# The scores of an indexer tile computed one tile ahead of its search, the first tile's in another buffer

## The chip, the cores and the metric

The kernel runs on one core of a Trainium2 chip. The metric is device time in microseconds (us), the median of the runs. One further execution was profiled, and all rows below are from it.

## The reference, cut to what matters

One step of a two-layer encoder over 592 tokens: 16 meta tokens and 512 prompt tokens (group i), and 64 sample tokens with a cache of 256 keys (group ii). Each layer has three branches. The change touches branch A alone, sparse attention behind an indexer:

```python
s_idx = relu(einsum('bthd,bsd->bths', qib, ki))       # 4 indexer heads of 64
score = einsum('bth,bths->bts', wib, s_idx)
score = where(k_chunk[None, :] <= qcb[:, None], score, -inf)
top_val, top_idx = lax.top_k(score, topk)             # 128 of the prompt's keys, 80 of the sample's
# softmax attention of 8 heads over the chosen keys alone
```

Branch B is a width-4 convolution and a gated linear recurrence (RG-LRU), branch C multi-scale pooling. Every projection is split into a high and a low part and takes three matmuls a step.

## The kernel before

**The main stream.** A layer projects chunk after chunk (`c_project`, 24 accumulating matmuls for each of two pieces of 296 or 288 columns, all on line 255, tile `acc`, three PSUM buffers). The order in the stretch that matters: two indexer query groups QI, four recurrence groups XB, four key groups K, four query groups Q, then the gates GB of branch B. A weight chunk is split by ACT (`wh`, L191) and DVE (`wl`, L192) three chunks ahead of its use. The result of a K or Q group is copied to SBUF by ACT and then gets its rotary part in `rope`: DVE shuffles (L354), POOL multiplies twice (L355 and L356), DVE adds (L357, into `QK`).

**Work at the side.** Generators in the list `side` (indexer and attention) and in `side_lru` (the recurrence of one group, L639 to L675: convolution into `lxc`, two gate matmuls `pg` on L653, ACT functions, two scans L671 and L672) are stepped a little after each piece of a projection. A scheduler then orders the instructions of each engine; every engine works through its own list in that order.

**The indexer.** `index(j)` handles one tile of 128 queries, j = 0 to 3, or the 64 sample queries, j = 4. For each of four heads a matmul (L432, L433 or L435, into `pq`, two PSUM buffers) is followed by a weighted ReLU that adds into the tile `sc` (L438, L442 on DVE, with ACT's ReLU into the tile `rel` between). Then the search repeats two DVE instructions, 16 times (10 for the sample): MAX finds the eight largest of a row, MATCH_REPLACE takes them out. In the profile a MATCH_REPLACE is two rows, MATCH_VALUE_LOAD and MATCH_REPLACE8. Tile 4 is 320 wide, tile 0 is 144 wide and 64 partitions high (partitions 64 to 127), tile 1 is 272 wide. The result is the tile `bias`, which attention adds to its logits. `sc` has one buffer, so the first score row of a tile (L438) waits for the last reader of `sc` of the tile before (L455).

**Who waits for DVE.** `attend_meta` (L596, layer 0 alone) and `attend(4)` (L500) read the `QK` that the L357 adds complete; `attend(4)` reads it through two copies on POOL (L474, into `VI`). A gate's piece leaves PSUM by L695 on DVE (tile `e`), and TensorE reuses that `acc` buffer three pieces later. Under TensorE's in-order list a matmul that waits holds all the matmuls behind it.

In row names PE is TensorE's matmul, DVE VectorE, ACT ScalarE, POOL GpSimd.

Of the kernel before, what the change touches and what calls it, by code (L numbers as in the profile page):

```python
# [9 lines left out]
F32 = mybir.dt.float32  # L10
# [7 lines left out]
NM = 16  # L18
# [49 lines left out]
def build(ctx, tc, ap):  # L68
# [9 lines left out]
    tmp = pool("tmp", 1)  # L78
# [48 lines left out]
    side = Side(RATE_ATT)  # L127
# [169 lines left out]
    def layer(l, xn, x_src, last):  # L297
# [61 lines left out]
        def rotated(ch, dst, pieces):  # L359
            def ev(i, c0, n, p):  # L360
                nc.scalar.activation(dst[:, c0:c0 + n], p, AF.Copy)
            c_project(ch, 8, xn, pieces, ev)
            rope(dst, pieces[0][0])
# [44 lines left out]
        def kspan(j):  # L408

            w = NM + 128 * (j + 1)  # L410
            if w <= 512:
                return [(0, w)]
            return [(0, w // 2), (w // 2, w // 2)]

        def index(j):
            sample = j == 4
            rows = 128
            q0 = NP if sample else NM + 128 * j
            w = 320 if sample else NM + 128 * (j + 1)
            sc = tmp.tile([128, 528], F32, name="sc", tag="sc")  # L420
            spans = [(0, 320)] if sample else kspan(j)
            nq = 64 if sample else 128
            for par in range(2):
                o = 64 * par
                for z in range(0, 128, nq):
                    nc.gpsimd.tensor_copy(qiz[o:o + 64, par::2, z:z + nq], QI[o:o + 64, 0:2, q0:q0 + nq])
            for h in range(4):
                q = qiz[:, h]
                for a, n in spans:
                    p = psq.tile([128, 512], F32, name="pq", tag="qk")  # L430
                    if sample:
                        nc.tensor.matmul(p[:, 0:256], lhsT=q, rhs=kx, start=True, stop=True)  # L432
                        nc.tensor.matmul(p[:, 256:320], lhsT=q, rhs=QI[:, 2, NP:NT], start=True, stop=True)  # L433
                    else:
                        nc.tensor.matmul(p[:, :n], lhsT=q, rhs=QI[:, 2, a:a + n], start=True, stop=True)  # L435
                    wh = wq[:rows, j, h:h + 1]
                    if h == 0:
                        nc.vector.tensor_scalar(sc[:rows, a:a + n], p[:rows, :n], 0.0, wh, op0=ALU.max, op1=ALU.mult)  # L438
                    else:
                        r = tmp.tile([128, 400], F32, name="rel", tag="rel")  # L440
                        nc.scalar.activation(r[:rows, :n], p[:rows, :n], AF.Relu)
                        nc.vector.scalar_tensor_tensor(sc[:rows, a:a + n], r[:rows, :n], wh, sc[:rows, a:a + n],  # L442
                                                       op0=ALU.mult, op1=ALU.add)
                yield w * 1.1
            if not sample:
                nc.gpsimd.memset(sc[0:64, w - 64:w], MASKED)  # L446
            r0 = 64 if j == 0 else 0
            rr = slice(r0, rows)
            m8 = sm.tile([128, 8], F32, name="m8", bufs=2)
            for _ in range(10 if sample else 16):  # L450
                nc.vector.max(m8[rr], sc[rr, :w])  # L451
                nc.vector.match_replace(sc[rr, :w], m8[rr], sc[rr, :w], TAKEN)  # L452
                yield w * 2.1 + 140
            b = lp.tile([128, 528], BF16, name="bias", tag="bias")
            nc.vector.tensor_scalar(b[rr, :w], sc[rr, :w], TAKEN, -1.0e30, op0=ALU.not_equal, op1=ALU.mult)  # L455
            if j == 0:
                nc.vector.memset(b[0:64, 0:w - 64], 0.0)
                nc.vector.memset(b[0:64, w - 64:w], -1.0e30)
            bias[j] = b
            yield w  # L460
# [311 lines left out]
        last_values()  # L772
        for i in range(2):
            rotated(s["c"][C_QI + i], QI[:, i], FULL)
        side.add(index(4))
        side.add(index(0))
        side.add(index(1))
        for g in range(4):
            c_project(s["c"][C_XB + g], 8, xn, FULL, ev_pad(XB[:, g], 3))
            side_lru.add(lru(g))  # L780
# [7 lines left out]
            side.add(attend_meta())  # L788
        side.add(attend(4))
        side.add(attend(0))  # L790
        side.add(index(2))
        side.add(attend(1))
        side.add(index(3))
        side.add(attend(2))
        side.add(attend(3))
        y = new_y()
# [92 lines left out]
    for t, (c0, rows) in enumerate(TILES):  # L889
# [9 lines left out]
        else:  # L899
            norm_T(x[t], rows, c0, r, (g0[:, 0:512], g0[:, 512:1024]), *xn)  # L900
    xn = layer(0, xn, ap["xin"], False)
    layer(1, xn, x1, True)


# [73 lines left out]
```

## Time and profile before

| | |
|---|---|
| median of 3 runs | 1241.58 us (1241.14 to 1242.72) |
| profiled execution, its own time | 1241.46 us |
| its span, first to last instruction | 1239.6 us |
| busy: PE, DVE, ACT, POOL | 1217.6, 731.9, 466.7, 321.4 us |
| mean granted TensorE clock | 0.997 of full speed |

The span plus 1.9 us is the execution's own time. A busy share of an engine is an average over the whole span; in a stretch it can be quite different.

### The profile page before, as it was taken

What the parts mean: (1) busy time and instruction counts of PE and PEld (TensorE: products, weight loads), DVE (VectorE), ACT (ScalarE), POOL (GpSimd) and SP (SyncE); (2) the same over time, 40 slices, a digit from 0 to 9 for tenths busy, and PEclk for the clock granted to TensorE, in tenths of its full rate; (3) what the DMA queues carried; (4) which work ended last, traced back from release to release, by engine and by line L of the source; (5) the groups of instructions that cost most, each with busy time, mean ns of one, the idle gap of its engine ahead of it and who ended that gap; (6) DMA issues with size and microseconds to landing.
All of it is one profiled execution on the core that took longest, in us unless ns stands there. A gap on an engine that the chain in (4) does not pass through costs nothing.

```text
span 1239.6 us, 20846 instructions
## 1 busy us (share of the span) xinstructions
PE 1217.6 (98%) x8314; PEld 1158.5 (93%) x8314; DVE 731.9 (59%) x1502; ACT 466.7 (38%) x913; POOL 321.4 (26%) x428
## 2 busy tenths in 40 slices
PE   9999899999999999999999998899999999999997
PEld 7999889999999999998799998899999999999975
DVE  6268995856954435343453789959497543344332
ACT  6345455333233323332343446443423432233322
POOL 2133454131144400011012334441221442101121
PEclk9999999999999999999999999999999999999999
DMA  8322231221222132222353222222122212222212
GB/s 284 121 74 69 91 108 55 69 69 60 91 76 68 57 93 82 85 74 81 114 160 117 69 68 97 89 69 69 52 94 77 79 52 91 76 81 86 86 35 77
DMA packets 39155, 106.79 MB, mean 86 GB/s; under 512 B 8177, under 2 KB 11313, under 8 KB 38802
## 3 DMA queue, kind: packets, MB, share of 16 engines
q1 hardware_dynamic: 38912, 105.40, 26.4%
q8 instruction: 65, 1.06, 0.3%
q14 instruction: 32, 0.26, 0.1%
q10 hardware_dynamic: 146, 0.07, 0.0%
HBM read 94.83 MB, written 10.09 MB: 85 GB/s over the span
## 4 chain that ended last, share of the span: by engine, by line
PE 87%; DVE 8%; issue 1%; DMA 1%; POOL 1%; ACT 1%; SPq 0%; POOLq 0%; DVEq 0%; ACTq 0%
PE acc L255 75%; PE pq L504 3%; PE pv L547 3%; PE pT L532 2%; DVE wl L192 1%; PE pq L435 1%; DVE sc L452 1%; DVE m L451 1%; DVE lxc L643 1%; DVE rt L354 1%; DVE QK L357 1%; PE pg L761 1%; DMA xi<-xin 1%; PE pT L564 1%; DVE CH L671 1%
## 5 line engine op out<-in xcount | busy, mean ns | idle before, releaser
L255 PE MATMUL acc<-xh,wh 128*128 128x296 f32 (+1 forms) x1728 | 528.5, 306 | 2.8 <-DVE e L695 2.8
L255 PE MATMUL acc<-xh,wl 128*128 128x296 f32 (+1 forms) x1728 | 523.3, 303 | 0.0
L255 PE MATMUL acc<-xl,wh 128*128 128x296 f32 (+1 forms) x1728 | 519.0, 300 | 0.0
L255 PEld LDWEIGHTS acc<-xh,wh 128*128 128x128 f32 x1728 | 326.7, 189 | 6.8 <-DVE e L695 3.0
L255 PEld LDWEIGHTS acc<-xl,wh 128*128 128x128 f32 x1728 | 326.8, 189 | 3.3
L255 PEld LDWEIGHTS acc<-xh,wl 128*128 128x128 f32 x1728 | 325.5, 188 | 2.0
L192 DVE TENSOR_TENSOR wl<-wr,wh 128x1024 fp32r<-128x1024 f32 (+1 forms) x158 | 208.9, 1327 | 200.5 <-ACT wh L191 194.0
L191 ACT ACTIVATE wh<-wr 128x1024 fp32r<-128x1024 f32 (+1 forms) x158 | 166.0, 1053 | 233.8 <-PE acc L255 189.3
L255 PE MATMUL acc<-yh,wh 128*128 128x296 f32 (+1 forms) x384 | 116.9, 304 | 0.0
L255 PE MATMUL acc<-yl,wh 128*128 128x296 f32 (+1 forms) x384 | 115.6, 301 | 0.0
L255 PE MATMUL acc<-yh,wl 128*128 128x296 f32 (+1 forms) x384 | 115.6, 301 | 0.0
L517 POOL TENSOR_SCALAR lpa<-lpa,mn 128x128 f32<-128x128 f32 (+4 forms) x72 | 81.8, 1136 | 109.4 <-DVE mn L516 100.6
L451 DVE MAX8 m<-sc 64x8 f32<-64x144 f32 (+4 forms) x148 | 74.7, 505 | 3.6 <-POOL sc L446 0.7
L255 PEld LDWEIGHTS acc<-yl,wh 128*128 128x128 f32 x384 | 72.2, 188 | 1.3 <-issue 0.2
L255 PEld LDWEIGHTS acc<-yh,wl 128*128 128x128 f32 x384 | 72.2, 188 | 1.2 <-issue 0.4
L255 PEld LDWEIGHTS acc<-yh,wh 128*128 128x128 f32 x384 | 72.3, 188 | 1.0
L452 DVE MATCH_REPLACE8 sc<-m,sc 64x144 f32<-64x144 f32 (+4 forms) x148 | 72.6, 490 | 0.2
L734 POOL TENSOR_TENSOR e<-m,e 128x592 f32<-128x592 f32 (+1 forms) x16 | 23.2, 1450 | 184.4 <-DVE e L728 184.4
L514 ACT ACTIVATE lpa<-lpa,mn 128x144 f32<-128x144 f32 (+4 forms) x72 | 41.2, 572 | 75.0 <-DVE mn L508 74.9
L719 ACT ACTIVATE e<-acc 128x296 f32<-128x296 f32 (+1 forms) x96 | 38.9, 405 | 65.0 <-PE acc L255 64.8
L255 PE MATMUL acc<-wh,ml 128*128 128x512 f32 (+2 forms) x160 | 63.2, 395 | 0.0
L255 PE MATMUL acc<-wh,mh 128*128 128x512 f32 (+2 forms) x160 | 62.8, 394 | 0.0
(209 smaller groups left out, 1639.9 us busy)
## 6 DMA issues: line engine op xcount, KB each, us to landing
wr<-wc SPq DMA_DIRECT2D x108, 512.0 KB, 3.5
wr<-wb SPq DMA_DIRECT2D x24, 512.0 KB, 3.5
wr<-wo SPq DMA_DIRECT2D x16, 512.0 KB, 3.8
kT<-QK SPq DMA_DIRECT2D x2, 1184.0 KB, 4.3
xi<-xin SPq DMA_DIRECT2D x8, 256.0 KB, 7.0
wr<-wv SPq DMA_DIRECT2D x4, 512.0 KB, 6.1
v_p<-VI SPq DMA_DIRECT2D x16, 128.0 KB, 2.1
xo<-xin SPq DMA_DIRECT2D x8, 256.0 KB, 3.1
```

The source lines that it names most:

```text
L191: nc.scalar.activation(h[:, :size], r[:, :size], AF.Copy)
L192: nc.vector.tensor_sub(lo[:, :size], r[:, :size], h[:, :size].bitcast(F32))
L255: nc.tensor.matmul(out, lhsT=a, rhs=b, start=(i == 0), stop=(i == n - 1))
L451: nc.vector.max(m8[rr], sc[rr, :w])
L452: nc.vector.match_replace(sc[rr, :w], m8[rr], sc[rr, :w], TAKEN)
L504: nc.tensor.matmul(p[:, :n], lhsT=qz[u // 2 % 2][:, u % 2], rhs=QK[:, 4 + u // 2, a:a + n], start=True, stop=True)
L514: nc.scalar.activation(t[:, :w], t[:, :w], AF.Exp, bias=mn[:, i:i + 1], scale=-1.0, accum_out=mn[:, 2:3])
L517: nc.gpsimd.tensor_scalar(t[:, :wm], t[:, :wm], mn[:, 3:4], None, op0=ALU.mult)
L532: nc.tensor.transpose(ps[:, k], t[:, 128 * k:128 * k + 128], ident)
L547: nc.tensor.matmul(pvs[i // 2][:, i % 2], lhsT=val(k, i), rhs=pt[:, k], start=(k == 0 and i % 2 == 0), stop=(k == nb - 1), skip_group_chec ...
L719: nc.scalar.activation(e[:, c0:c0 + nn], p, AF.Tanh, scale=0.5)
L734: nc.gpsimd.tensor_tensor(e[:, C0:], m[:, j, C0:], e[:, C0:], op=ALU.add)
```

## The change

`index(j)` is cut in two generators. `scores(j)` computes the scores, `search(j)` searches them. In the list the scores of tile 0 now stand ahead of the search of tile 4, and the scores of tile 1 ahead of the search of tile 0. The scores of tile 0 go into the buffer of the tag `pt`, which attention uses later, all others into `sc` as before. No instruction is added or removed; the lines of the profile move by 3 (L438 becomes L441, L442 L445), by 9 from the search on (L357 keeps its number, L451 becomes L460, L452 L461, L643 L652, L695 L704), and by 14 behind the list.

```diff
--- before.py
+++ after.py
@@ -412,12 +412,15 @@
                 return [(0, w)]
             return [(0, w // 2), (w // 2, w // 2)]
 
-        def index(j):
+        score = {}
+
+        def scores(j):
             sample = j == 4
             rows = 128
             q0 = NP if sample else NM + 128 * j
             w = 320 if sample else NM + 128 * (j + 1)
-            sc = tmp.tile([128, 528], F32, name="sc", tag="sc")
+
+            sc = score[j] = tmp.tile([128, 528 if j else 1024], F32, name="sc", tag="sc" if j else "pt")
             spans = [(0, 320)] if sample else kspan(j)
             nq = 64 if sample else 128
             for par in range(2):
@@ -444,6 +447,12 @@
                 yield w * 1.1
             if not sample:
                 nc.gpsimd.memset(sc[0:64, w - 64:w], MASKED)
+
+        def search(j):
+            sample = j == 4
+            rows = 128
+            w = 320 if sample else NM + 128 * (j + 1)
+            sc = score.pop(j)
             r0 = 64 if j == 0 else 0
             rr = slice(r0, rows)
             m8 = sm.tile([128, 8], F32, name="m8", bufs=2)
@@ -772,9 +781,12 @@
         last_values()
         for i in range(2):
             rotated(s["c"][C_QI + i], QI[:, i], FULL)
-        side.add(index(4))
-        side.add(index(0))
-        side.add(index(1))
+        side.add(scores(4))
+        side.add(scores(0))
+        side.add(search(4))
+        side.add(scores(1))
+        side.add(search(0))
+        side.add(search(1))
         for g in range(4):
             c_project(s["c"][C_XB + g], 8, xn, FULL, ev_pad(XB[:, g], 3))
             side_lru.add(lru(g))
@@ -788,9 +800,11 @@
             side.add(attend_meta())
         side.add(attend(4))
         side.add(attend(0))
-        side.add(index(2))
+        side.add(scores(2))
+        side.add(search(2))
         side.add(attend(1))
-        side.add(index(3))
+        side.add(scores(3))
+        side.add(search(3))
         side.add(attend(2))
         side.add(attend(3))
         y = new_y()
```

**What stands where on DVE now.** The first place is the end of the search of tile 4 (`sc_889`) in layer 0. Before:

```order
L452 MATCH_REPLACE sc_889<-m8_943,sc_889 128x320
L451 MAX m8_943<-sc_889 128x8
L452 MATCH_REPLACE sc_889<-m8_943,sc_889 128x320
L451 MAX m8_943<-sc_889 128x8
L452 MATCH_REPLACE sc_889<-m8_943,sc_889 128x320
L455 TENSOR_SCALAR bias_1175<-sc_889 128x320
L457 MEMSET bias_1450 64x40
L458 MEMSET bias_1450 64x64
L438 TENSOR_SCALAR sc_1177<-pq_1180,wq_317 128x144
```

and now, with the rows of tile 0 (`sc_943`, 64 partitions):

```order
L460 MAX m8_965<-sc_889 128x8
L461 MATCH_REPLACE sc_943<-m8_1284,sc_943 64x144
L461 MATCH_REPLACE sc_889<-m8_965,sc_889 128x320
L460 MAX m8_1284<-sc_943 64x8
L460 MAX m8_965<-sc_889 128x8
L461 MATCH_REPLACE sc_943<-m8_1284,sc_943 64x144
L461 MATCH_REPLACE sc_889<-m8_965,sc_889 128x320
L460 MAX m8_1284<-sc_943 64x8
L460 MAX m8_965<-sc_889 128x8
```

Before, a MAX and the MATCH_REPLACE that needs it followed each other, and the scores of tile 0 (`sc_1177`) came behind the search of tile 4; now the rows of two searches alternate.

The second place is the rotary add of the last Q group in layer 0 (`QK_312<-QK_312,rt_1889`). Before:

```order
L451 MAX m8_1516<-sc_1454 128x8
L695 SCALAR_TENSOR_TENSOR e_1903<-e_1903,acc_1910 128x296
L669 SCALAR_TENSOR_TENSOR lT_1879<-lT_1879,lthi_1871 128x595
L452 MATCH_REPLACE sc_1454<-m8_1516,sc_1454 128x272
L671 SCALAR_TENSOR_TENSOR CH_314<-la_1878,lT_1879 128x528
L672 SCALAR_TENSOR_TENSOR CH_314<-la_1878,prm_108,lT_1879 128x64
L451 MAX m8_1516<-sc_1454 128x8
L357 TENSOR_TENSOR QK_312<-QK_312,rt_1889 128x592
L452 MATCH_REPLACE sc_1454<-m8_1516,sc_1454 128x272
L192 TENSOR_TENSOR wl_2090<-wr_1800,wh_2089 128x1024
L451 MAX m8_1516<-sc_1454 128x8
```

and now:

```order
L192 TENSOR_TENSOR wl_1992<-wr_1726,wh_1991 128x1024
L354 STREAM_SHUFFLE rt_1889<-QK_312 128x592
L460 MAX m8_1516<-sc_1234 128x8
L674 SCALAR_TENSOR_TENSOR lthi_1871<-lthi_1871,lxc_1758 128x595
L461 MATCH_REPLACE sc_1234<-m8_1516,sc_1234 128x272
L678 SCALAR_TENSOR_TENSOR lT_1879<-lT_1879,lthi_1871 128x595
L704 SCALAR_TENSOR_TENSOR e_1903<-e_1903,acc_1910 128x296
L680 SCALAR_TENSOR_TENSOR CH_314<-la_1878,lT_1879 128x528
L681 SCALAR_TENSOR_TENSOR CH_314<-la_1878,prm_108,lT_1879 128x64
L357 TENSOR_TENSOR QK_312<-QK_312,rt_1889 128x592
L192 TENSOR_TENSOR wl_2090<-wr_1800,wh_2089 128x1024
```

Before, 9 MAX and 8 MATCH_REPLACE rows of tile 1 (`sc_1454`) stand ahead of the add and 15 behind it; now all 32 (`sc_1234`) stand ahead. The other rows from the row at 86.81 us on that stand ahead of it are the same in both lists.

The third place is the same add in layer 1 (`rt_8070`), with the gate row of `acc_8091` ahead of it. Before:

```order
L669 SCALAR_TENSOR_TENSOR lT_8062<-lT_8062,lthi_8054 128x595
L695 SCALAR_TENSOR_TENSOR e_8084<-e_8084,acc_8091 128x288
L451 MAX m8_7699<-sc_7637 128x8
L671 SCALAR_TENSOR_TENSOR CH_6536<-la_8061,lT_8062 128x528
L672 SCALAR_TENSOR_TENSOR CH_6536<-la_8061,prm_108,lT_8062 128x64
L452 MATCH_REPLACE sc_7637<-m8_7699,sc_7637 128x272
L357 TENSOR_TENSOR QK_6534<-QK_6534,rt_8070 128x576
L451 MAX m8_7699<-sc_7637 128x8
L192 TENSOR_TENSOR wl_8361<-wr_7982,wh_8360 128x1024
L695 SCALAR_TENSOR_TENSOR e_8084<-e_8084,acc_8152 128x288
```

and now:

```order
L674 SCALAR_TENSOR_TENSOR lthi_8054<-lthi_8054,lxc_7941 128x595
L460 MAX m8_7699<-sc_7417 128x8
L678 SCALAR_TENSOR_TENSOR lT_8062<-lT_8062,lthi_8054 128x595
L704 SCALAR_TENSOR_TENSOR e_8084<-e_8084,acc_8091 128x288
L461 MATCH_REPLACE sc_7417<-m8_7699,sc_7417 128x272
L680 SCALAR_TENSOR_TENSOR CH_6536<-la_8061,lT_8062 128x528
L681 SCALAR_TENSOR_TENSOR CH_6536<-la_8061,prm_108,lT_8062 128x64
L357 TENSOR_TENSOR QK_6534<-QK_6534,rt_8070 128x576
L192 TENSOR_TENSOR wl_8361<-wr_7982,wh_8360 128x1024
L704 SCALAR_TENSOR_TENSOR e_8084<-e_8084,acc_8152 128x288
L814 SCALAR_TENSOR_TENSOR e_8084<-CH_6536,e_8084 128x512
```

Of tile 1's 32 search rows (`sc_7637`, now `sc_7417`) 16 stood ahead of the add before; now all 32 do.

On TensorE the matmuls of the last head in `attend_meta` stand behind 978 accumulating matmuls of the layer's stream (987 before), and the first of `attend(4)` in layer 1 behind 4650 of the program's (4653 before).

## Rows read from the trace of the kernel before

**Rows 1.** Timeline of PE, its five waits: start us, us, instruction [idle before <-releaser].
```profile
143.31 1.28 PE L435 MATMUL pq<-VI,qiz 128*128 128x272 f32 x2 [3.14 <-DVE sc L438]
...
175.51 0.22 PE L596 MATMUL pq<-QK 64*16 64x16 f32 x4 [1.83 <-DVE QK L357]
...
755.97 0.73 PE L435 MATMUL pq<-VI,qiz 128*128 128x272 f32 x2 [3.27 <-DVE sc L438]
...
786.12 0.40 PE L255 MATMUL acc<-xh,wh 128*128 128x288 f32 x1 [2.75 <-DVE e L695]
...
790.73 0.70 PE L500 MATMUL pq<-CH,VI 128*128 128x256 f32 x2 [1.55 <-POOL VI L474]
```

**Rows 2.** Windows, two stretches: us, busy (x count) by engine, PEclk, DMA share, GB/s.
```profile
145.00:180.00 35.00, 33.17 (x242) 32.20 (x241) 34.66 (x71) 17.03 (x26) 21.05 (x23) 0.98 0.30 99
755.00:795.00 40.00, 34.73 (x243) 33.26 (x243) 39.45 (x76) 16.77 (x27) 20.18 (x23) 1.00 0.28 98
```

**Rows 3.** Windows, six us behind the first wait.
```profile
142.00:148.00 6.00, 4.69 (x21) 4.46 (x22) 5.97 (x12) 1.08 (x4) 0.64 (x2) 0.72 0.51 188
```

**Rows 4.** Timeline of DVE, layer 0: waits of the score rows, and layer 1's.
```profile
110.22 0.42 DVE L442 SCALAR_TENSOR_TENSOR sc<-rel,wq,sc 128x144 f32<-128x144 f32 x1 [2.48 <-ACT rel L441]
...
722.85 0.44 DVE L442 SCALAR_TENSOR_TENSOR sc<-rel,wq,sc 128x144 f32<-128x144 f32 x1 [2.46 <-ACT rel L441]
```

**Rows 5.** Timeline of DVE, the add of the last Q group, layers 0 and 1.
```profile
174.71 0.75 DVE L357 TENSOR_TENSOR QK<-QK,rt 128x592 f32<-128x592 f32 x1
...
788.13 0.74 DVE L357 TENSOR_TENSOR QK<-QK,rt 128x576 f32<-128x576 f32 x1
```

**Rows 6.** Timeline of DVE, search rows 128 partitions high and their neighbours.
```profile
157.73 0.09 DVE L452 MATCH_VALUE_LOAD sc<-m,sc 128x8 f32 x1
...
158.27 0.44 DVE L451 MAX8 m<-sc 128x8 f32<-128x272 f32 x1
158.63 1.51 DVE L192 TENSOR_TENSOR wl<-wr,wh 128x1024 fp32r<-128x1024 f32 x1
...
166.75 0.08 DVE L452 MATCH_VALUE_LOAD sc<-m,sc 128x8 f32 x1
...
167.17 1.22 DVE L192 TENSOR_TENSOR wl<-wr,wh 128x1024 fp32r<-128x1024 f32 x1
...
168.31 0.85 DVE L354 STREAM_SHUFFLE rt<-QK 128x592 f32<-128x592 f32 x1
```

**Rows 7.** Timeline of DVE, a search row 64 partitions high behind a wl row.
```profile
133.11 1.23 DVE L192 TENSOR_TENSOR wl<-wr,wh 128x1024 fp32r<-128x1024 f32 x1
134.37 0.09 DVE L452 MATCH_VALUE_LOAD sc<-m,sc 64x8 f32 x1
```

**Rows 8.** The chain that ended last: start us, us, what.
```profile
297.26 18.70 PE acc L255 x137
```

**Rows 9.** Timeline of DVE and of PE, the third XB group of layer 0.
```profile
125.20 0.84 DVE L643 SCALAR_TENSOR_TENSOR lxc<-CH,prm,lxc 128x595 f32<-128x595 f32 x1
...
130.38 1.17 PE L653 MATMUL pg<-lxc,bd 128*128 128x298 f32 x4
```

**Rows 10.** Groups on DVE from 86 to 176 us: busy us, mean ns | idle.
```profile
L643 DVE SCALAR_TENSOR_TENSOR lxc<-CH,prm,lxc 128x595 f32<-128x595 f32 x9 | 9.4, 1042 | 0.1
L671 DVE TENSOR_TENSOR_SCAN CH<-la,lT 128x528 f32<-128x528 f32 x4 | 7.1, 1780 | 0.0
```

**Rows 11.** Groups on DVE from 697 to 789 us.
```profile
L643 DVE SCALAR_TENSOR_TENSOR lxc<-CH,prm,lxc 128x595 f32<-128x595 f32 x9 | 10.6, 1177 | 0.1
L669 DVE SCALAR_TENSOR_TENSOR lT<-lT,lthi 128x595 f32<-128x595 f32 x4 | 5.1, 1285 | 0.8 <-ACT lT L668 0.7
L671 DVE TENSOR_TENSOR_SCAN CH<-la,lT 128x528 f32<-128x528 f32 x4 | 5.0, 1245 | 0.0
L666 DVE SCALAR_TENSOR_TENSOR lT<-lthr,lT 128x595 f32<-128x595 f32 x4 | 3.1, 773 | 0.1
```

**Rows 12.** Timeline of POOL, second rope product of the first Q group.
```profile
149.32 2.42 POOL L356 TENSOR_TENSOR QK<-QK,rope_c 128x592 f32<-128x592 f32 x1
```

## The prediction

> **What bounds the kernel now.** I read the page's shares first: TensorE is busy for 98% of the span, so only its few waits can be given back. Its timeline has five of note before 800 us, all in the two stretches where an indexer works beside the Q groups and the first gate pieces, one in each layer [rows 1]. The reader is to see the releaser at the end of each row: DVE ends four of them and the fifth comes over POOL's copies of a tile that DVE completes. Two are what the change addresses: the score matmuls of tile 1 (L435) find no free `pq`, because the score row L438 waits for `sc`, which tile 0's search still holds, 3.14 us in layer 0 and 3.27 us in layer 1. The wait in layer 0 has a tail: in the six us around it the granted clock is 0.72, part of the stretch at 1.2 GHz in place of 2.4, which is worth (1 - 0.72) · 6 = 1.7 us [rows 3]; in layer 1 the mean is 1.00 [rows 2]. Together 3.14 + 1.7 + 3.27 = 8.1 us.
>
> Next I asked whether the one that TensorE waits for has time to spare. It has none: DVE is busy for 34.66 of 35 us and 39.45 of 40 us [rows 2]. TensorE stalls at `sc`, but had it not, it would have come earlier to the next matmul that needs DVE, and waited there. So in these stretches DVE is the bound, and the time is set by how much DVE work stands in its list ahead of the row that frees TensorE last. In both layers that is the rotary add L357 of the last Q group [rows 5]: `attend_meta` waits for it 1.83 us in layer 0, `attend(4)` through POOL 1.55 us in layer 1 [rows 1]. Behind them TensorE has no other wait of such size, so from there on the end follows its restart one for one.
>
> **The change, part by part.** It removes no DVE row and adds none. I counted, from the first row of tile 4's scores in each layer on, what stands ahead of the add in the old and the new list.
>
> *More search ahead of the add.* In layer 0, 9 MAX and 8 MATCH_REPLACE of tile 1 stood ahead, now 16 and 16: 7 and 8 more. In layer 1, 8 and 8 more. All else ahead of it is the same. What such a row costs is the distance to the next start where that next row is independent: MAX 158.63 - 158.27 = 0.36 us; MATCH_REPLACE with its load 167.17 - 166.75 = 0.42 us [rows 6]. Layer 0: 7 · 0.36 + 8 · 0.42 = 5.9 us. Layer 1: 8 · 0.36 + 8 · 0.42 = 6.2 us.
>
> *Alternating searches.* A dependent row costs more: from MATCH_VALUE_LOAD to its MAX it is 158.27 - 157.73 = 0.54 us, against 0.42 us, so 0.11 to 0.12 us a dependence [rows 6]. Two searches in turn remove it where their rows lie on the same partitions. But tile 0 is 64 partitions high, and a row of it behind an independent row of 128 partitions starts only 1.26 us after that one's start, though it lasts 1.23 us, where rows of equal height overlap: a `wl` of 1.22 us is followed after 1.14 us [rows 6, 7]. In the new list layer 0 has 31 dependent neighbours fewer and 27 changes of height more, net 4 · 0.11 = 0.4 us gained; layer 1 has 28 fewer and 27 more, 0.1 us. What is left is +5.5 and +6.1 us.
>
> The Trainium skill, page "VectorE: DVE Perf Modes", section "The DRAIN you can't avoid", has the next operation start only when the pipe is empty, an operation that nothing holds excepted. Were every row held, no order would change a row's cost: the rows would count in full, 0.47 us for a MAX and 0.54 us for a MATCH_REPLACE, and the forecast by it would be about 1254 us. The trace agrees with the exception for rows of equal height, which start 0.08 us before the end of the one ahead.
>
> *DVE's idle gap.* Before, DVE stood still for 2.48 us and 2.46 us at a tile 0 score row, since ACT's `rel` came late from a late matmul [rows 4]. The scores of tile 0 are issued much earlier now, with the whole search of tile 4 behind them, which covers ACT. So the gap goes. The add moves by 5.5 - 2.5 = +3.0 us in layer 0, and by 6.1 - 2.5 = +3.6 us in layer 1. If another gap of that size takes its place, each layer loses 2.5 us more.
>
> *TensorE's list.* Behind the restart stand the matmuls that were done before it in the old list. 978 main matmuls precede the last head of `attend_meta`, before 987: 9 · 0.1365 = 1.2 us of work moves behind it, a matmul taking 18.70 / 137 us in a stretch without waits [rows 8]. In layer 1 it is 4650 against 4653: 0.4 us. Sum: layer 0 3.0 + 1.2 = 4.2, layer 1 3.6 + 0.4 = 4.0, together +8.2 us.
>
> *Where the stalls move.* The two waits at `sc` go, and others stand in their place. The third XB group's last `lxc` row ends at 126.04 us, and its gate matmuls start at 130.38 us [rows 9]; in the new list 11.6 us more of DVE rows stand ahead of it, less the 2.5 us gap: ready near 135.2 us, and TensorE, behind which all later matmuls queue, is there near 131 us. It waits about 4.4 us; some less at the fourth group; then at the last head of `attend_meta` for the add, which starts near 177.7 us in place of 174.71 us. In layer 1 the same, with the add near 791.8 and the restart at 790.73 + 3.6 = 794.3 us. Another buffer costs nothing by itself: the first attention writes `pt` only long after the search of tile 0. The `wl` splits are three chunks ahead, and a delay of 3 to 5 us stays inside that.
>
> **The rivals.**
>
> *The change does what it says and nothing takes the place of the waits*: 1241.46 - 8.1 = 1233.4 us. It needs DVE to have slack between the waits, which rows 2 exclude; a chance of 0.05.
>
> *The other side: fewer collisions, faster or no change.* A DVE row that reads two tiles is longer while POOL runs the rotary products, such as the one of 2.42 us [rows 12]. In layer 0 the nine convolution rows L643 take 1.042 us on average where a free one takes 0.84 us [rows 9, 10], and the scans L671 1.780 us, where layer 1 has 1.245 us [rows 10, 11]. Search rows read one tile; if in the new list they are what runs beside POOL, this goes: layer 0 9 · 0.20 + 4 · 0.535 = 3.9 us, layer 1 9 · (1.177 - 0.84) + 4 · (1.285 - 0.773) = 5.0 us (L669 against the equal row L666 [rows 11]), together 8.9 us: 1249.7 - 8.9 = 1240.8 us. It decides from 8.2 us on, nearly all of it. Against it: three of the four products of each layer still have rows of the recurrence beside them in the new list. A chance of 0.08 for most of it; a third of it, 3 us, I allow in the range.
>
> The Trainium skill, page "SBUF — State Buffer", section "Who interferes with whom", names a port that DVE with two SBUF inputs and GpSimd share; the 1.042 against 0.840 us agree with it.
>
> *Alternating rows overlap at unequal height too*: then 27 · 0.11 = 3.0 us less a layer, 1249.7 - 6.0 = 1243.7 us, within the 2.5 us (0.2%) that a measurement can tell from no change. For it: nothing in the list makes the rows wait for each other. Against it: rows 7. A chance of 0.10.
>
> The Trainium skill, page "VectorE: DVE Perf Modes", section "Two Vector instructions with no wait between them", has the second one held when the start quadrant of its input or output differs from that of the last; by that rule, too, the alternation gains little, and the 1.26 us agree.
>
> *Worse*: a wait of some 4 us at the third XB group brings the lower clock again, as the 3.14 us did, 1.7 us in each of one or two layers, or a gap of 2.5 us takes the place of the one that went: 1252 to 1255 us. A chance of 0.13.
>
> **How the numbers follow.** The profiled execution took 1241.46 us, 0.1 us under the median, so the sum holds for both: 1241.46 + 8.2 = 1249.7 us. A chance of 0.64 for this, give or take 3 us; with *worse* it makes 0.77 slower. Within 0.2%, 1239.1 to 1244.1 us, lie the overlap at unequal height, 0.10, and a part of the collisions' rival, 0.03. Faster are the first rival, 0.05, and the rest of the collisions' rival, 0.05. The range reaches down to 1243.0 us, to the overlap's case, and up to 1255 us; it leaves out faster cases and the tail of *worse*.
>
> **What would show it.** Right: no wait of TensorE on a score row; DVE busy for over 97% up to the add in both layers; all 32 search rows of tile 1 done when the add starts, near 177.7 and 791.8 us; a wait of some 4 us at L662 of the third XB group; the gap at `rel` gone; rows of 64 and 128 partitions in turn without overlap. Wrong: if the add starts no later than before, the rows cost less in turn or the collisions fell; if it starts later and the total does not follow, TensorE had other work to do or another wait further back took it up; if TensorE waits long where DVE is idle, an order that I took as covered (ACT's `rel`, POOL's copies) has become the limit.

## The result

The changed kernel takes 1254.15 us, median of 4 runs (1252.88 to 1256.29), against 1241.8 us before: a ratio of 1.010, 95% interval 1.0088 to 1.0112, so 12.4 us slower. The forecast was 1249.7 us, in a range of 1243 to 1255. One of the five executions of e5 below took 6820.65 us; its median counts it, its ratio does not.

The profile after, first TensorE's timeline, the waits of 0.8 us and more at the two places where [rows 1] had five, and one of 0.56 us:

```profile
136.90 2.25 PE L662 MATMUL pg<-lxc,bd 128*128 128x298 f32 x4 [4.59 <-DVE lxc L652]
...
163.43 1.49 PE L662 MATMUL pg<-lxc,bd 128*128 128x298 f32 x4 [2.99 <-DVE lxc L652]
...
181.34 0.22 PE L605 MATMUL pq<-QK 64*16 64x16 f32 x4 [1.32 <-DVE QK L357]
...
756.38 2.35 PE L662 MATMUL pg<-lxc,bd 128*128 128x298 f32 x4 [4.65 <-DVE lxc L652]
...
781.18 1.27 PE L662 MATMUL pg<-lxc,bd 128*128 128x298 f32 x4 [0.87 <-DVE lxc L652]
...
798.07 0.40 PE L255 MATMUL acc<-xh,wh 128*128 128x288 f32 x1 [1.81 <-DVE e L704]
...
802.39 1.22 PE L509 MATMUL pq<-CH,VI 128*128 128x256 f32 x2 [0.56 <-POOL VI L483]
```

The waits of over 3 us at `sc` are gone, as the change says; 0.65 and 0.66 us of them are left, at 111.03 and 730.52 us. In their place TensorE waits for `lxc`, at the third XB group and again at the fourth, and still for the last Q add. DVE ends every wait again, the last one over POOL.

Windows of the changed kernel: both stretches up to the add, the six us around the first long wait, and the four us behind the restart in layer 1.

```profile
140.00:182.00 42.00, 37.69 (x263) 36.14 (x263) 41.01 (x82) 22.72 (x34) 22.06 (x21) 0.95 0.31 111
755.00:800.00 45.00, 40.94 (x268) 39.10 (x269) 43.86 (x90) 24.58 (x36) 23.66 (x22) 0.92 0.33 113
136.00:142.00 6.00, 5.10 (x22) 4.46 (x23) 5.78 (x15) 3.71 (x5) 2.57 (x3) 0.72 0.26 91
802.00:806.00 4.00, 3.61 (x12) 3.25 (x13) 3.10 (x9) 1.56 (x4) 0.57 (x3) 0.50 0.44 131
```

The third figure of each row is DVE: 41.01 of 42 and 43.86 of 45 us, saturated as in [rows 2]. The clock behind the new wait is 0.72, the value of [rows 3] behind the old one; and in layer 1 TensorE restarts at 0.50, where the mean over the whole stretch was 1.00 before [rows 2].

TensorE's own account has the loss as well. Its waits in the two stretches sum to 12.5 us before [rows 1] and to 18.1 us now (the rows above and the two at `sc`), +5.6 us. By the mean granted clock of the span, 0.997 and 0.990, the lower clock costs 3.7 and 12.5 us, +8.8 us. Together that is 14.4 us for the 13.6 us by which the span grew, and the larger part of it is clock. Most of what the clock costs seems not to add to the time, though: of the four executions of the changed kernel those at 0.988 and 0.995 differ by 8.8 us in what the clock costs and by 2.9 us in time (1256.29 and 1253.35). That fits a DVE that sets the add, since a TensorE that comes later then waits less for it; only the clock behind the add adds to the time.

DVE's own timeline, the gap at `rel` and the two adds that answer to [rows 4, 5]:

```profile
92.97 0.37 DVE L445 SCALAR_TENSOR_TENSOR sc<-rel,wq,sc 128x144 f32<-128x144 f32 x1 [0.95 <-ACT rel L444]
...
180.54 0.74 DVE L357 TENSOR_TENSOR QK<-QK,rt 128x592 f32<-128x592 f32 x1
...
799.76 0.73 DVE L357 TENSOR_TENSOR QK<-QK,rt 128x576 f32<-128x576 f32 x1
```

To set each layer's share apart I take the first rotary add of a layer, on the indexer's keys, as its start. DVE's timeline has it in the changed kernel at

```profile
61.85 0.76 DVE L357 TENSOR_TENSOR VI<-VI,rt 64x592 f32<-64x592 f32 x1
...
681.36 0.75 DVE L357 TENSOR_TENSOR VI<-VI,rt 64x592 f32<-64x592 f32 x1
```

and before at

```profile
61.58 0.76 DVE L357 TENSOR_TENSOR VI<-VI,rt 64x592 f32<-64x592 f32 x1
...
674.26 0.75 DVE L357 TENSOR_TENSOR VI<-VI,rt 64x592 f32<-64x592 f32 x1
```

Layer 0, start to start, is 619.51 us long after and 612.68 us before: +6.8 us. From layer 1's start to the end of the span (1253.2 and 1239.6 us) it is 571.8 and 565.3 us: +6.5 us. The last Q add stands 118.69 us behind the start in layer 0 (113.13 before), +5.6 us, and 118.40 us in layer 1 (113.87), +4.5 us. What lies between add and layer is the matmuls moved behind it and, in layer 1, the half clock.

### The profile page after: what moved, and what is told of

Read it like the earlier page. It is cut to its first block, busy times and chain, and to the rows that moved or that the text cites. A ratio compares the mean times of both kernels' runs of the same rounds, so it can differ in the third digit from the quotient of the medians.

```text
span 1253.2 us, 20854 instructions
## 1 busy us (share of the span) xinstructions
PE 1225.4 (98%) x8314; PEld 1164.7 (93%) x8314; DVE 734.3 (59%) x1502; ACT 467.7 (37%) x913; POOL 321.0 (26%) x428
## 4 chain that ended last, share of the span: by engine, by line
PE 82%; DVE 14%; issue 2%; POOL 1%; DMA 1%; ACT 0%; SPq 0%; POOLq 0%; DVEq 0%; ACTq 0%
PE acc L255 70%; PE pq L513 3%; PE pv L556 3%; DVE sc L461 3%; DVE m L460 2%; DVE wl L192 2%; DVE lxc L652 2%; PE pT L541 2%; DVE rt L354 1%; PE pq L438 1%; DVE lT L678 1%; DVE QK L357 1%; PE pg L770 1%; PE pT L243 1%; DVE CH L680 1%
## 5 line engine op out<-in xcount | busy, mean ns | idle before, releaser
L460 DVE MAX8 m<-sc 64x8 f32<-64x144 f32 (+4 forms) x148 | 74.8, 505 | 3.8 <-POOL sc L449 1.0
L461 DVE MATCH_REPLACE8 sc<-m,sc 64x144 f32<-64x144 f32 (+4 forms) x148 | 72.8, 492 | 0.5
```

## The experiments

Theory 1: the time follows the last Q add, and that follows the DVE work ahead of it in DVE's list. Theory 2: the time was lost where the new waits stand, at the third XB group. By size theory 2 fits too: 4.6 + 1.7 us, twice, is 12.6 us. Theory 3: all DVE work of the stretch counts, wherever it stands. Each ratio is to the kernel before, run on the same chip.

**e1, two buffers in the old order.** The list of the change put back:

```diff
         side.add(scores(4))
-        side.add(scores(0))
         side.add(search(4))
-        side.add(scores(1))
+        side.add(scores(0))
         side.add(search(0))
+        side.add(scores(1))
         side.add(search(1))
```

> The two generators and the second buffer stay, the list is put back in the old order: search of tile 4 ahead of the scores of tile 0, search of tile 0 ahead of the scores of tile 1. By the instruction order 28 rows of tile 1's search stand ahead of the last Q add in layer 0 and 27 in layer 1 (17 and 16 before, 32 after the change), and the third XB group's convolution row comes about 8 us earlier in DVE's list than after the change. Theory 1 (the DVE work ahead of the last Q add sets the time): the add comes 1.6 to 2.1 us a layer earlier than after the change, 1249 to 1251 us. Theory 2 (the time was lost in the new waits at the third XB group's gates, 4.6 us a layer and the lower clock behind them): these waits go, 4.6 + 1.7 us a layer come back, 1241 to 1242 us.

Measured: 1250.68 us, ratio 1.0061 (1.0049 to 1.0074). TensorE's timeline, layer 0:

```profile
127.81 1.24 PE L438 MATMUL pq<-VI,qiz 128*128 128x272 f32 x2 [1.97 <-DVE sc L441]
...
160.12 1.27 PE L662 MATMUL pg<-lxc,bd 128*128 128x298 f32 x4 [2.73 <-DVE lxc L652]
...
180.06 0.24 PE L605 MATMUL pq<-QK 64*16 64x16 f32 x4 [3.67 <-DVE QK L357]
```

and a window behind the restart:

```profile
180.00:186.00 6.00, 5.94 (x27) 5.91 (x28) 5.90 (x20) 1.01 (x2) 0.95 (x3) 0.51 0.31 90
```

The third group's wait, at 136.90 us in the changed kernel, is gone, and of the 12.4 us only 4.4 came back, as theory 1 had it: theory 2 falls as the whole cause. In layer 0 TensorE waits longer for the add, 3.67 us. But a wait for `lxc` has moved to the fourth group, 2.73 us above and more in layer 1:

```profile
779.30 1.87 PE L662 MATMUL pg<-lxc,bd 128*128 128x298 f32 x4 [4.47 <-DVE lxc L652]
```

So e1 alone does not exclude that waits for `lxc`, at whichever group, are the loss; e3 does. Also, the second buffer by itself makes two thirds of the loss: once tile 1's scores need not wait for tile 0's search, the scheduler lifts tile 1's search ahead of the add (28 and 27 rows).

**e2, half of tile 1's search.**

```diff
-            for _ in range(10 if sample else 16):
+            for _ in range(10 if sample else 8 if j == 1 else 16):
```

> The changed kernel with 8 of the 16 steps of tile 1's search left out, so half of that search is not computed. 16 DVE rows fewer stand ahead of the last Q add, none fewer ahead of the third XB group. Theory 1: the add comes 7.0 us a layer earlier; the waits at the third and fourth XB groups stay and are then the last, so not all of it comes back: 1243 to 1250 us. Theory 2 (the third XB group's waits are the loss): nothing comes back, 1254 us.

Measured: 1253.43 us, ratio 1.0087 (1.0072 to 1.0103). A miss for theory 1 as I had put it: 16 rows fewer, 7 us by the list, and the adds come only 1.4 and 2.7 us earlier. Where the time went stands on DVE, in layer 0:

```profile
164.34 0.78 DVE L357 TENSOR_TENSOR QK<-QK,rt 128x592 f32<-128x592 f32 x1 [2.76 <-POOL QK L356]
...
170.09 0.78 DVE L357 TENSOR_TENSOR QK<-QK,rt 128x592 f32<-128x592 f32 x1 [3.09 <-POOL QK L356]
...
179.29 0.74 DVE L357 TENSOR_TENSOR QK<-QK,rt 128x592 f32<-128x592 f32 x1
```

DVE now stands idle at the adds of two Q groups for POOL's products; the search rows had filled that time. Layer 0 is even 0.7 us longer than in the changed kernel: behind TensorE's restart at 180.09 us the clock is 0.72 over six us, 1.7 us, where the changed kernel has 1.00. Under the list lies a second limit, the chain shuffle, two POOL products, add, once a group. Rows put ahead of the add cost in full where DVE is busy; rows taken away give back only what is not such filling.

**e7, the same with half of POOL's rotary work.** It tests that reading; the second product is left out.

```diff
-            nc.gpsimd.tensor_tensor(x[:, c0:], x[:, c0:], rope_c[:r, c0:], op=ALU.mult)
```

> The kernel of e2, half of tile 1's search left out, and in the rotary part the second product on POOL left out too (so keys and queries are not rotated rightly). In e2 DVE stood 2.76 and 3.09 us at the adds of two Q groups for POOL. Theory 1 in the form that e2 leaves (search rows only fill the time in which DVE would wait for POOL; the last add then ends a chain of shuffles, POOL products and adds): the two waits shrink to some 1.3 to 1.6 us, the last add comes 3 to 4 us earlier than in e2, 1246 to 1249 us. Theory 2 (TensorE's progress since the third XB group's wait sets the add): as e2, 1253 us.

Measured: 1240.81 us, ratio 0.9984 (0.9975 to 0.9993), less than I expected. DVE's timeline (line numbers one lower):

```profile
160.77 0.78 DVE L356 TENSOR_TENSOR QK<-QK,rt 128x592 f32<-128x592 f32 x1 [1.58 <-POOL rt L355]
...
165.08 0.78 DVE L356 TENSOR_TENSOR QK<-QK,rt 128x592 f32<-128x592 f32 x1 [1.65 <-POOL rt L355]
```

The waits shrink to 1.58 and 1.65 us, as the chain requires. The rest has other sources. Groups of DVE rows from the first search to the add in layer 0, first of e2, then of e7:

```profile
L652 DVE SCALAR_TENSOR_TENSOR lxc<-CH,prm,lxc 128x595 f32<-128x595 f32 x9 | 10.3, 1150 | 0.2
```

```profile
L651 DVE SCALAR_TENSOR_TENSOR lxc<-CH,prm,lxc 128x595 f32<-128x595 f32 x9 | 7.5, 832 | 0.0
```

With half of the products gone the convolution rows fall from 1150 to 832 ns, their free value [rows 9]. And in these stretches the clock falls below 1.00 in one place only, about 750 us, where e2 has it in four. So e7 shows that POOL's products set these two waits, but not how much is theirs of the 11.6 us between e2 and e7 (+10.7 and -0.9 us, each against the kernel before on its chip): the collisions, the clock and TensorE's wait at the third XB group (4.57 us in e2, 2.84 us here, layer 0) ease with them. For that reason e7 does not decide against theory 2 either. The Trainium skill, page "SBUF — State Buffer", section "Who interferes with whom", has a DVE row with two SBUF inputs and a GpSimd row that reads SBUF contend for one port; the 1150 against 832 ns agree.

**e6, eight more steps of tile 1's search.**

```diff
-            for _ in range(10 if sample else 16):
+            for _ in range(10 if sample else 24 if j == 1 else 16):
```

> The changed kernel with 24 steps of tile 1's search in place of 16 (it takes out 192 values a row, which is not what is asked for). 16 DVE rows a layer more; by the order only one or two more of them stand ahead of the last Q add, all others behind it. Theory 1 (what stands ahead of the add counts): 0.4 to 0.8 us a layer, 1254 to 1256 us. Theory 3 (any DVE work of the stretch counts): 7 us a layer, 1267 us.

Measured: 1253.19 us, ratio 1.0086 (1.0071 to 1.0102). Some 14 rows a layer behind the add cost nothing: theory 3 falls. The adds stand 0.7 and 0.3 us later than in the changed kernel, from the start of their layer, as the one or two rows ahead of them ask; in the total that is lost in the spread.

**e3, tile 0 on all partitions.**

```diff
-            r0 = 64 if j == 0 else 0
+            r0 = 0
```

> The changed kernel with tile 0 searched on all 128 partitions, so that rows of two searches in turn have the same height; the same number of rows, each as long. By the order 54 changes of height a layer ahead of the last add go. Theory 1 with my price of 0.11 us for a change of height: 6.4 us a layer earlier, 1241 to 1243 us. If a change of height costs nothing: 1254 us.

Measured: 1244.2 us, ratio 1.0012 (1.0003 to 1.0021): 10 us back with the same number of rows, 1 us less than I expected. One step of both searches in turn, on DVE's timeline; first the changed kernel (a row of x2 is two MAX rows), then e3:

```profile
104.34 0.09 DVE L461 MATCH_VALUE_LOAD sc<-m,sc 64x8 f32 x1
...
104.78 0.09 DVE L461 MATCH_VALUE_LOAD sc<-m,sc 128x8 f32 x1
...
105.40 0.83 DVE L460 MAX8 m<-sc 64x8 f32<-64x144 f32 x2
...
106.27 0.09 DVE L461 MATCH_VALUE_LOAD sc<-m,sc 64x8 f32 x1
```

```profile
104.53 0.07 DVE L461 MATCH_VALUE_LOAD sc<-m,sc 128x8 f32 x1
...
104.80 0.08 DVE L461 MATCH_VALUE_LOAD sc<-m,sc 128x8 f32 x1
...
105.26 0.69 DVE L460 MAX8 m<-sc 128x8 f32<-128x144 f32 x2
...
105.87 0.07 DVE L461 MATCH_VALUE_LOAD sc<-m,sc 128x8 f32 x1
```

The step takes 106.27 - 104.34 = 1.93 us at unequal height and 105.87 - 104.53 = 1.34 us at equal height: 0.59 us for four changes of height, 0.15 us each. Over the whole stretch the adds come 4.4 and 5.2 us earlier than in the changed kernel for 54 changes, 0.08 to 0.10 us each, so the 0.15 us hold for the tight alternation alone. The Trainium skill, page "VectorE: DVE Perf Modes", section "Two Vector instructions with no wait between them", holds an instruction whose start quadrant differs from that of the last; the two steps agree.

Tile 0 differs from the other tiles in height and in its first partition, 64. Rows of the changed kernel part the two. The indexer's keys are 64 partitions high too, but begin at partition 0:

```profile
61.13 0.83 DVE L354 STREAM_SHUFFLE rt<-VI 128x592 f32<-128x592 f32 x1
61.85 0.76 DVE L357 TENSOR_TENSOR VI<-VI,rt 64x592 f32<-64x592 f32 x1
```

The row of 64 partitions, the add of the keys, does not need the shuffle ahead of it, which is of a query group, and starts 61.13 + 0.83 - 61.85 = 0.11 us before its end. So unequal height alone does not keep rows from overlapping. By these rows it is the other first partition that costs at tile 0, and "height", in the prediction and here, stands for it; no run searched a tile of 64 partitions that begins at 0.

e3 also answers theory 2. TensorE's waits for `lxc` are still there, only at other sizes:

```profile
132.50 1.27 PE L662 MATMUL pg<-lxc,bd 128*128 128x298 f32 x4 [1.43 <-DVE lxc L652]
...
158.83 2.31 PE L662 MATMUL pg<-lxc,bd 128*128 128x298 f32 x4 [4.41 <-DVE lxc L652]
...
747.58 1.27 PE L662 MATMUL pg<-lxc,bd 128*128 128x298 f32 x4 [1.51 <-DVE lxc L652]
...
773.44 2.35 PE L662 MATMUL pg<-lxc,bd 128*128 128x298 f32 x4 [4.38 <-DVE lxc L652]
```

They sum to 11.7 us, against 13.1 us in the changed kernel and 7.2 us in e1, and against the kernel before on the same chip the three lose 1.5, 12.4 and 8.0 us. The loss does not follow these waits, at the third group or at any; it follows the adds.

**e5 and e8, the kernel before with tile 0 on all partitions.** The same one-line edit, in the kernel before; e8 repeats it for its profile.

> The kernel before, with tile 0 searched on all 128 partitions in place of 64. The same rows, each as long, without the 28 changes of height a layer ahead of the last Q add; the order then holds 6 rows of tile 1 ahead of the add in place of 17 and 16. Theory 1 with a price for a change of height: tile 0's search ends some 3 us earlier, so the wait at sc (3.14 and 3.27 us) is nearly gone and the lower clock behind it, and the wait for the add shrinks; the list alone would give 8 us a layer, but DVE then has to wait for POOL's rotary products as in e2 and e4 (2.7 to 3.1 us each), so 4 to 6 us a layer: 1230 to 1236 us. If a change of height costs nothing: 1242.7 us.

> The kernel of e5 once more, for a profile of an undisturbed execution: 1235 to 1238 us. Theory 1 expects in it: no wait over 0.7 us at the sc rows, the lower clock around 144 us gone, some 6 rows of tile 1 ahead of the last Q add and DVE standing 2.7 to 3.1 us for POOL at the adds of one or two Q groups.

Measured: 1236.72 and 1237.8 us, ratios 0.9953 (0.9938 to 0.9967) and 0.9957 (0.9942 to 0.9971): with e10 the fastest version here, 5 us ahead of the kernel before; e5 lies just above its expected range and e8 inside its own. In e8 TensorE's timeline shows the waits that I had expected to go:

```profile
152.71 0.72 PE L435 MATMUL pq<-VI,qiz 128*128 128x272 f32 x2 [2.74 <-DVE sc L438]
...
174.45 0.22 PE L596 MATMUL pq<-QK 64*16 64x16 f32 x4 [1.73 <-DVE QK L357]
...
765.95 0.73 PE L435 MATMUL pq<-VI,qiz 128*128 128x272 f32 x2 [2.48 <-DVE sc L438]
```

They stay, at 2.74 and 2.48 us, and the kernel is faster all the same: the adds come 2.0 and 3.6 us earlier than before, from the start of their layer. The expectation was wrong on the place and right on what sets the time. Six rows of tile 1 stand ahead of the add in each layer, as expected, against 17 and 16 before; so the gain comes from the changes of height and from the shorter list, and e8 does not part the two. At one Q add of layer 0 DVE waits for POOL, 2.79 us, as in e2.

**e4 and e9, tile 1's search behind the last Q add**, in the changed kernel and in e3.

```diff
-            if not sample:
+            if not sample and j != 1:
                 nc.gpsimd.memset(sc[0:64, w - 64:w], MASKED)
...
+            if j == 1:
+                nc.gpsimd.tensor_scalar(sc[0:64, w - 64:w], QK[0:64, 3, C0:C0 + 64], 0.0, MASKED,
+                                        op0=ALU.mult, op1=ALU.add)
...
-        side.add(search(1))
...
         side.add(attend(4))
+        side.add(search(1))
```

> The changed kernel with the search of tile 1 put behind the last Q add: its mask row on POOL reads one value of the added tile, and the generator stands behind attend(4). The same computation. No row of tile 1's search stands ahead of the add any more, while the third XB group's convolution row stays where the change put it. Theory 1: the add no longer holds TensorE, the waits at the third XB group stay, 0.65 + 4.6 + 1.7 us in layer 0 and about 8.7 us with the lower clock in layer 1, against 6.7 and 7.6 us before: 1242 to 1245 us. Theory 2: the third XB group's waits are unchanged and so is the time, 1254 us.

> The kernel of e4 (changed kernel, tile 1's search behind the last Q add) with tile 0 searched on 128 partitions. If only DVE's list ahead of the add counted, it would be free of some 20 us a layer and TensorE the only bound, 1229 us. With the chain of shuffle, POOL products and add behind it, as in e2 and e4, DVE stands idle in their place: 1237 to 1243 us. Theory 2: the third XB group's wait is 1.4 us as in e3, and the time that of e3, 1244 us, or less.

Measured: 1246.61 us, ratio 1.0037 (1.0023 to 1.0051), and 1240.49 us, 0.9981 (0.9972 to 0.9990). In e4 the adds come back to +0.2 and -1.0 us against the kernel before, yet layer 0 stays 4.5 us longer; a window behind its restart at 176.72 us shows one reason:

```profile
176.00:184.00 8.00, 7.28 (x38) 7.25 (x38) 5.36 (x14) 1.19 (x3) 2.53 (x4) 0.59 0.23 79
```

(1 - 0.59) · 8 = 3.3 us at the lower clock. The scheduler also set the rows of the third XB group differently, so its wait did not stay as I had expected; e4 is therefore no clean test of theory 2, and e1 and e3 have to carry that. e9 lands inside the range for the chain and 11 us above what the list alone would give. Its DVE timeline has waits for POOL at three adds of layer 0, one of them

```profile
157.40 0.83 DVE L357 TENSOR_TENSOR QK<-QK,rt 128x592 f32<-128x592 f32 x1 [2.77 <-POOL QK L356]
```

**e10, one rotary product on DVE**, in the kernel of e5.

```diff
-            nc.gpsimd.tensor_tensor(x[:, c0:], x[:, c0:], rope_c[:r, c0:], op=ALU.mult)
+            nc.vector.tensor_tensor(x[:, c0:], x[:, c0:], rope_c[:r, c0:], op=ALU.mult)
```

> The kernel of e5 with the second rotary product (by the cosines) on DVE instead of POOL, the same computation. Theory 1 with the POOL chain: each add waits for one product of 1.5 to 2 us in place of two, and 8 rows of some 0.75 us a layer fill DVE's waits; with POOL's second product its collisions with DVE go too: 1231 to 1236 us. If the 6 us of DVE rows a layer are work on the bound: 1243 to 1248 us.

Measured: 1237.16 us, ratio 0.9955 (0.9938 to 0.9972), the time of e8, between the two expectations. DVE's waits for POOL at the Q adds are gone and eight rows stand in their place; the experiment does not say which of the two would win elsewhere.

The adds and layers of all runs with comparable rows, against the kernel before, each from the start of its layer (us):

| kernel | add, layer 0 | layer 0 | add, layer 1 | layer 1 to the end |
|---|---|---|---|---|
| changed | +5.6 | +6.8 | +4.5 | +6.5 |
| e1 | +3.7 | +6.6 | +2.5 | +2.2 |
| e2 | +4.2 | +7.5 | +1.8 | +4.1 |
| e3 | +1.1 | +2.4 | -0.7 | -0.2 |
| e4 | +0.2 | +4.5 | -1.0 | +2.6 |
| e6 | +6.3 | +6.8 | +4.8 | +4.1 |
| e8 | -2.0 | -0.6 | -3.6 | -3.9 |
| e9 | -3.6 | -1.8 | -4.5 | -1.4 |

A layer is its add's shift plus -0.7 to 4.3 us. Most of the large rests is the clock behind the restart: 2.9 us of e1's layer 0 (0.51 over 6 us), 1.7 us of e2's and 3.3 us of e4's.

## Why the prediction was right, and by how much it was off

The measured time lies 0.85 us below the upper end of the range. The main forecast, 1249.7 us give or take 3 us, missed it; 1254.15 us stand where the prediction had put *worse*, 1252 to 1255 us, with a chance of 0.13. The mechanism is the one of the forecast, and its terms came out larger.

*DVE is the bound, not the waits at `sc`.* Right. The changed kernel has no long wait at `sc` and is slower; e8 has two and is faster. The place at which TensorE waits does not tell what costs.

*The stalls move.* Right in place and size: 4.4 us were forecast at the third XB group, 4.59 and 4.65 us came; less at the fourth, 2.99 and 0.87 us; then the add. The size owes something to luck: in layer 0 TensorE came at 132.31 and not 131 us, and the wait ended at 136.90 and not 135.2 us, so that two misses cancel. Two of the signs that the prediction named failed: a score row still holds TensorE, for 0.65 and 0.66 us, and the gap at `rel` is not gone.

*The adds.* Late by 5.6 and 4.5 us where the sum had 3.0 and 3.6 us. Three terms were mis-sized. The gap at `rel` did not go whole: DVE is early enough at 92.97 us to wait 0.95 us there. Its waits up to the add sum to 3.2 and 3.5 us before and to 1.3 and 1.3 us after, so 1.9 and 2.1 us came back, not 2.5. Alternating rows at unequal height gain nothing, not even the net 0.4 and 0.1 us: a step of each search for itself takes 1.12 us (tile 4, before, MAX to MAX) and 0.75 us (tile 0, where it stands alone), 1.87 us together; in turn they take 1.34 us at equal height and 1.93 us at unequal. A dependence removed is worth 0.13 us, a change of height costs 0.15 us, and not 0.11 both. And the collisions, which I had left as they were, grew in layer 0. Groups of DVE up to the add, before (lines not among [rows 10]) and after:

```profile
L669 DVE SCALAR_TENSOR_TENSOR lT<-lT,lthi 128x595 f32<-128x595 f32 x4 | 3.7, 914 | 0.8 <-ACT lT L668 0.7
L665 DVE SCALAR_TENSOR_TENSOR lthi<-lthi,lxc 128x595 f32<-128x595 f32 x4 | 3.1, 772 | 0.1
L672 DVE TENSOR_TENSOR_SCAN CH<-la,prm,lT 128x64 f32<-128x64 f32 x4 | 2.5, 617 | 0.0
```

```profile
L652 DVE SCALAR_TENSOR_TENSOR lxc<-CH,prm,lxc 128x595 f32<-128x595 f32 x9 | 11.2, 1241 | 0.2
L678 DVE SCALAR_TENSOR_TENSOR lT<-lT,lthi 128x595 f32<-128x595 f32 x4 | 6.1, 1536 | 0.0
L680 DVE TENSOR_TENSOR_SCAN CH<-la,lT 128x528 f32<-128x528 f32 x4 | 5.0, 1246 | 0.0
L674 DVE SCALAR_TENSOR_TENSOR lthi<-lthi,lxc 128x595 f32<-128x595 f32 x4 | 4.3, 1080 | 0.0
L681 DVE TENSOR_TENSOR_SCAN CH<-la,prm,lT 128x64 f32<-128x64 f32 x4 | 1.3, 328 | 0.0
```

The scans came free, as the rival of fewer collisions had it (7.1 to 5.0, 2.5 to 1.3 us), and three other kinds of rows took their place beside POOL: 9.4 to 11.2, 3.7 to 6.1 and 3.1 to 4.3 us. Net, from the means, 9 · 0.199 + 4 · (0.622 + 0.308 - 0.534 - 0.289) = +2.2 us, of which smaller changes on other lines take back 0.7; in layer 1 these lines give +0.3 us, and the others take it back. Counted from start to start on DVE's timeline, less the waits, as the prediction priced its rows, the search rows up to the add take 6.85 and 7.46 us more than before, where the sum had 5.5 and 6.1 us, and all other rows together +0.65 and -0.77 us, since more of them overlap their neighbours now. With the 1.9 and 2.1 us of waits that makes the 5.6 and 4.5 us. So the collisions' rival failed where I had doubted it: collisions move, they don't vanish. (Its two parts add to 9.0 us, not 8.9.)

*TensorE's list.* 1.2 us were forecast behind the add in layer 0, and 6.8 - 5.6 = 1.2 us came. In layer 1 it was 0.4 us, and 6.5 - 4.5 = 2.0 us came: the rest is the half clock at the restart, where the first main matmul follows the first of `attend(4)` after 2.58 us (802.39 to 804.97) and not 1.33 us as before (790.73 to 792.06). The rival *worse* had such a term, 1.7 us, but behind the third XB group. There the clock fell too (0.72 over six us), ahead of the add, where TensorE waits less for coming later. It is a term for the restart that was missing from the sum.

*Alternating rows overlap at unequal height*, the rival within no change: wrong, by e3. *Were every row held*, the prediction's figure of about 1254 us: right by its number alone, since rows that begin at the same partition overlap (the 0.08 us of the prediction, the 1.34 us of e3's step), and e3 is 10 us faster with the same rows.

*What the argument lacked.* It took DVE's saturation as work that could be counted in both directions. It holds for work that is added; of the 7 us a layer that e2 takes away only 1.4 and 2.7 us come back, because POOL's chain lies just under it. And *another buffer costs nothing by itself* is true of waits on the buffer alone: in e1 the buffer without the new order makes 8.0 of the 12.4 us, through the search rows that it lets come up DVE's list.

What stays open: how the shares of e7 divide between the shorter chain and fewer collisions, and why the clock falls behind one wait and not behind another of the same length (3.14 and 3.27 us before, [rows 1 to 3]).

## What to carry to other kernels

A wait of the bounding engine names the place where lateness is handed over, not its cause: if the engine it waits for is busy all through, a freed buffer lets other work come up that engine's list, and the row that is waited for next comes later. Count the rows ahead of that row in the new order; what is added there costs in full, but before you count on rows taken away, look for the chain that they were filling. Two searches in turn hide each other's latency only where their rows begin at the same partition, and making the smaller tile as high as the other cost nothing in row time here (a MAX of 144 columns takes 0.31 us on 64 partitions and 0.30 us on 128, in e3).

## What the runs showed of the hardware that I had not expected

A DVE row that begins at another partition than the row ahead of it costs 0.15 us in a tight alternation (0.59 us for four), enough to use up all that the alternation saves; a row of other height that begins at the same partition overlaps the row ahead (by 0.11 us, at 61.85 us of the changed kernel). A DVE row with two SBUF inputs grows, averaged over a stretch with POOL at work, by half (L652, 1241 ns in the changed kernel, where the equal row takes 832 ns in e7) or to the double (L678, 1536 ns, where the equal row L666 took 773 [rows 11]), and which rows are hit changes with the order alone. TensorE came back at the half clock from some waits of 1.4 us (e9, at 164.09 us; 0.72 over the six us from 164 us on) to 4.65 us, or fell back to it within two us, which cost up to 3.3 us, and from others not: 3.27 us before, in layer 1, left the mean at 1.00 [rows 2].
